# Sliding-window attention in a two-layer hybrid trunk: eight heads per tile, probabilities turned by VectorE and DRAM instead of TensorE

## The chip, the cores and the metric

The kernel runs on one core of a Trainium2 chip. The metric is the device time of one execution in microseconds (us); smaller is better. A core has TensorE (matrix multiply, "PE" in the profile, with "PEld" for its weight loads), VectorE (DVE), ScalarE (ACT), GpSimd (POOL) and SyncE (SP). Each takes its own instructions in the order in which the built program holds them. TensorE writes to PSUM, which here is eight banks of 128 partitions by 512 words; the others work on SBUF and PSUM (POOL on SBUF alone), and SyncE issues nearly all DMAs.

## The reference

Two layers, 1024 tokens, model width 1024, all float32. Each layer projects the normalised input into the inputs of three head groups (windowed attention, retention, gated linear attention), gates each group's output, and projects the concatenation back. The change is in the attention group alone:

```python
ATTN_HEADS = 8; ATTN_KV_HEADS = 2; HEAD_DIM = 64; WINDOW = 128; ATTN_BLOCK = 128
def sliding_window_attention(q, k, v, sinks):          # S = 1024, 8 blocks of 128
    kk, vv = with_prev(kb), with_prev(vb)              # each block sees itself and the one before
    s = jnp.einsum('bnqhgd,bnkhd->bnhgqk', qb, kk) * (D ** -0.5)
    s = jnp.where(valid, s, -1e30)                     # 0 <= i + 128 - j < WINDOW
    p = jax.nn.softmax(jnp.concatenate([s, sink], axis=-1), axis=-1)[..., :-1]
    return jnp.einsum('bnhgqk,bnkhd->bnqhgd', p, vv)
...
a_out = sliding_window_attention(aq, ak, av, sinks) * jax.nn.silu(ag)
y = jnp.concatenate([a_out, r_out, g_out], axis=-1) @ w_out
```

For one query the window holds exactly 128 keys: those above its place in the previous block and those up to its place in its own. So 128 probabilities per query and head are enough, one from each key position, previous or own.

## The kernel before

The tokens are eight tiles of 128 (t = 0 to 7), and two halves (hf) of four tiles. The eight heads are two groups g of four; inside a group the two heads of a pair j lie in partitions 0 to 63 and 64 to 127 (r = 0, 1). A float32 operand is split where precision allows it into a rounded high part and the rest, and a product takes three passes (`PASSES`: high x high, low x high, high x low) in the faster `fp32r` form; transposes and value products run in plain float32.

The order on TensorE is written by a planner inside the kernel: `mult` and `transp` add estimated costs to a clock `clk`, long matrix products call `pump()` every few matmuls, and `pump` lets waiting jobs (generators) go on whose due time has come. A job yields a delay (`lat(key, l)`, from the table `L`, with own values for layer 1 under `@1`) or a flag that another job sets. The planner never waits on the chip: it only decides the order. The other engines' order follows the order of emission, moved by the framework's scheduler where buffers and operands allow it.

Around the attention a layer runs, in this order: the projections of retention and linear attention; key and value projections `do_kv(p)` for tile pairs, with the keys turned by TensorE (`attn_kv`) into `kT`; the rotations `attn_rot(l, hf, g)`, each two projections of 24 matmuls of 512 columns, multiplied by sine and cosine on VectorE, with two 32-partition blocks of each pair exchanged by DMA on SyncE; the gate projections (`gate`, eight in all: two halves, two groups, two k each); and the output projection, which first loads the mixture of a tile (`load_mix`, or parts of it in the last layer's `last_output`, where pairs of tiles share seven products).

In the attention job `attn_q(l, t, g, q)` one group of four heads of one tile goes through: 12 score matmuls into two banks (L911); previous-block scores copied by ACT and own-block scores by VectorE under a mask (L918 to L920); maximum (L922), four exponentials with sums (L925), reciprocal (L928), normalisation on POOL (L929); then, after `aq3`, four TensorE transposes (L934), a copy by ACT, a mask on POOL (L940); after `aq4` the value products (L946), two column halves of TensorE at a time: `va` is v of the previous tile with all probabilities, `vd` the difference of the two tiles' v with the masked ones; a copy and a store to `aoS` in DRAM. q is split into high and low once per half and group, by `split_later`, 5 to 6 us after the rotation, into a tile `mq` of the `mx` ring.

The gates wait for the four tiles of their half and group (flags `ao`), load `aoS` from DRAM, multiply, split, and store to `mixS` (and `mixF` in the last layer); `load_mix` waits for those. Pools: `t2` (128 x 512 words) has B2 = 10 buffers, `t1` B1 = 8, `smx` SMB = 3, and of the eight PSUM banks three are `mm` (projections) and five `aux` (all else).

Of the kernel before, what the change touches and what calls it, by code (L numbers as in the profile page):

```python
# [17 lines left out]
P = 128  # L18
# [42 lines left out]
def host_constants():  # L61
# [9 lines left out]
    c["mask2"] = ((i[:, None] <= i[None, :]) & (i[:, None] // 32 == i[None, :] // 32)).astype(np.int32)  # L71
    c["curmask"] = (i[:, None] >= i[None, :]).astype(np.int32)
# [21 lines left out]
def trunk(ctx: ExitStack, tc: tile.TileContext, ins, cst, out):  # L94
# [167 lines left out]
    srS = dr.tile([NT, P, 256], F32, name="srS")  # L262
    tabS = dr.tile([NP_, P, 2, 256], F32, name="tabS")
# [501 lines left out]
    curmask = cload("curmask", I32)  # L765
    rmask = cload("rmask")
# [74 lines left out]
    def split_later(mq, q, name):  # L841
        yield lat("aq6", name[1])
        for j in range(2):
            split(mq[:, 0, j], mq[:, 1, j], q[j])
        flag(name, lat("aq2", name[1]))

# [12 lines left out]
    def attn_rot(l, hf, g, w_):  # L859
# [15 lines left out]
        q = w  # L875
        for j in range(2):
            A.activation(q[j], u[j], AF.Copy)
            for r in range(2):
                dst, src = 64 * r + 32 * (1 - j), 64 * r + 32 * j
                dma("qst", q[j][dst:dst + 32], u[1 - j][src:src + 32])  # L880
        mq = mix_tile().rearrange("p a k q -> p (a k q)").rearrange("p (a j n) -> p a j n", a=2, j=2)
        kv[(hf, g)] = mq
        job(split_later(mq, q, ("q", l, hf, g)))

    def attn_run(l):

        for hf in range(2):
            for g in range(2):
                for t in range(4 * hf, 4 * hf + 4):
                    yield (lat("aq7" if hf else "aq1", l), ("q", l, hf, g))  # L890
                    yield (0.0, ("kT", l, t))
                    job(attn_q(l, t, g, kv[(hf, g)]))

    def attn_q(l, t, g, q):

        sm = gp.tile([P, 4, 129], F32, tag="smx", name=nm("smx"), bufs=SMB)
        V.tensor_copy(sm[:, :, 128], sink8[:, l, 4 * g:4 * g + 4])
        if t == 0:
            G.memset(sm[:, :, 0:128], -1e30)
        else:  # L900
            vd = gp.tile([P, P], F32, tag="vd", name=nm("vd"), bufs=3)
            G.tensor_tensor(vd, kv["v"][t], kv["v"][t - 1], ALU.subtract)
        pss = [aux(), aux()]
        n = P if t == 0 else 2 * P
        cols = slice((t + 1) * P - n, (t + 1) * P)
        for j in range(2):
            qc = slice(P * (t % 4), P * (t % 4) + P)
            for i, (a, b) in enumerate(PASSES):
                for r in range(2):
                    rr = slice(64 * r, 64 * r + 64)  # L910
                    mult(pss[r][:, j * n:(j + 1) * n], q[rr, a, j, qc], kv["kT"][b][rr, cols],  # L911
                         i == 0, i == 2, n / 4600.0)
        if t % 4 == 3:
            flag(("s", l, t // 4, g))
        for r in range(2):
            pv = pss[r][:, 0:2 * n].rearrange("p (j c n) -> p j c n", j=2, n=P)
            sv = sm[:, r:4:2, 0:128]
            if t > 0:  # L918
                copy("sprev", sv, pv[:, :, 0, :])
            V.copy_predicated(sv, curmask.unsqueeze(1).to_broadcast((P, 2, P)), pv[:, :, n // P - 1, :])  # L920
        mx = small(4)
        V.tensor_reduce(mx, sm, AX.X, ALU.max, negate=True)  # L922
        sums = small(4)
        for h in range(4):
            A.activation(sm[:, h, :], sm[:, h, :], AF.Exp, bias=mx[:, h:h + 1],  # L925
                         accum_out=sums[:, h:h + 1])
        rs = small(4)
        V.reciprocal(rs, sums)  # L928
        eng("pn").tensor_tensor(sm[:, :, 0:128], sm[:, :, 0:128], rs.unsqueeze(2).to_broadcast((P, 4, P)), ALU.mult)  # L929
        yield lat("aq3", l)  # L930

        pp = aux()
        for h in range(4):
            transp(pp[:, h * P:(h + 1) * P], sm[:, h, 0:128], ident)  # L934
# [787 lines left out]
```

## Time and profile before

| what | us |
|---|---|
| median of three runs | 997.67 (996.91 to 997.82) |
| the profiled execution's own time | 996.31 |
| its span, first to last instruction | 994.6 |
| TensorE busy | 965.7 |
| VectorE busy | 683.2 |
| ACT busy | 409.3 |
| POOL busy | 246.3 |

A row of the profile names line, engine, operation, result and operands, the shape, a count, and then busy time in us, mean ns of one, and the idle time of the engine before them with what ended it. In the timeline the first number is the start and the second how long the merged group took; matmuls overlap, so the distance between two starts is the price on TensorE. A window row gives length and busy time of PE, PEld, DVE, ACT and POOL with instruction counts, then granted clock, DMA share and GB/s. A DMA row gives the count, the size, and the median time from issue to landing.

### The profile page before, as it was taken

Reading aid. Unit: us, or ns where it says so; the run is one execution under the profiler, and the core shown is the slowest. Engines: PE = TensorE matmul, PEld = TensorE weight load, DVE = VectorE, ACT = ScalarE, POOL = GpSimd, SP = SyncE. Lnnn points to the kernel's source line nnn. Section 1 sums busy time; section 2 is a strip of 40 time slices with the busy share of each in tenths; the row PEclk is TensorE's granted clock in tenths of the full one; section 3 lists DMA queues with packets and bytes.
Section 4 is the critical chain, followed back from the end, with each engine's and each line's share of the span. In section 5 each row is a group of like instructions: output and inputs, shape, how many; then the busy total and the mean of one; then the engine's idle time right before and its main releaser. Section 6 shows DMA issues by size and latency. Waiting matters only on the chain.

```text
span 994.6 us, 19641 instructions
## 1 busy us (share of the span) xinstructions
PE 965.7 (97%) x7133; PEld 824.3 (83%) x7133; DVE 683.2 (69%) x1679; ACT 409.3 (41%) x1152; POOL 246.3 (25%) x310
## 2 busy tenths in 40 slices
PE   5899999999999999999999999999999999999996
PEld 1599999888998777778889999988999877777785
DVE  3779857677766777664677286775766577567876
ACT  2477312233332656632555332133333257574222
POOL 2322001233310234420124101113322034545000
PEclk8899999999999999999999999999999999999999
DMA  9843513523135355587555241352122434378883
GB/s 321 290 138 97 159 44 115 177 86 121 61 100 166 91 157 168 170 274 239 189 170 171 69 150 38 118 157 83 53 93 86 127 91 133 112 235 266 267 262 139
DMA packets 112305, 148.77 MB, mean 150 GB/s; under 512 B 12065, under 2 KB 63821, under 8 KB 112209
## 3 DMA queue, kind: packets, MB, share of 16 engines
q1 hardware_dynamic: 106512, 137.96, 44.5%
q10 hardware_dynamic: 5696, 9.56, 2.6%
q8 instruction: 56, 0.92, 0.4%
q14 instruction: 41, 0.33, 0.1%
HBM read 109.20 MB, written 36.18 MB: 146 GB/s over the span
## 4 chain that ended last, share of the span: by engine, by line
PE 80%; DVE 7%; DMA 7%; issue 2%; POOL 1%; ACT 1%; SPq 0%; ACTq 0%; POOLq 0%; DVEq 0%
PE mm L165 61%; PE aux L165 14%; PE aux L180 5%; DMA st<-in_w_in_dram 2%; POOL sm L635 1%; DMA t<-aoS 1%; DMA st<-in_w_last_dram 1%; DMA xk<-in_x_dram 1%; DVE arena L533 1%; DMA a<-mixS 1%; DVE t L1248 0%; DVE t L328 0%; DMA t<-in_x_dram 0%; DMA t<-xs 0%; DMA mixS<-t 0%
## 5 line engine op out<-in xcount | busy, mean ns | idle before, releaser
L165 PE MATMUL mm<-arena 128*128 128x256 f32 (+2 forms) x1824 | 299.9, 318 | 1.8 <-ACT arena L704 1.8
L165 PE MATMUL mm<-arena,arena 128*128 128x256 f32 (+2 forms) x1824 | 298.2, 316 | 0.0
L165 PEld LDWEIGHTS mm<-arena 128*128 128x128 f32 x1824 | 255.5, 191 | 26.0 <-issue 3.3
L165 PEld LDWEIGHTS mm<-arena,arena 128*128 128x128 f32 x1824 | 252.2, 188 | 24.3 <-issue 3.7
L635 POOL TENSOR_TENSOR sm<-sm,mhalf 128x1 f32<-128x1 f32 (+1 forms) x64 | 55.8, 872 | 335.9 <-DVE sm L634 317.8
L165 PE MATMUL mm<-arena,mx 128*128 128x512 f32 (+1 forms) x564 | 130.6, 387 | 0.5 <-ACT kept L1341 0.5
L165 PEld LDWEIGHTS mm<-arena,mx 128*128 128x128 f32 x564 | 101.4, 188 | 24.7 <-issue 1.9
L149 ACT ACTIVATE t<-aux 128x256 f32<-128x256 f32 (+2 forms) x124 | 55.8, 468 | 73.8 <-PE aux L180 62.2
L149 ACT ACTIVATE arena<-st 128x512 fp32r<-128x512 f32 x94 | 56.2, 627 | 53.2 <-DMA st<-in_w_in_dram 19.4
L929 POOL TENSOR_TENSOR smx<-smx,sm 128x512 f32<-128x512 f32 x32 | 36.1, 1129 | 125.7 <-DVE sm L928 118.0
L533 POOL TENSOR_TENSOR arena<-st,arena 128x512 fp32r<-128x512 f32 x31 | 42.7, 1378 | 79.7 <-ACT arena L149 72.9
L533 DVE TENSOR_TENSOR arena<-st,arena 128x512 fp32r<-128x512 f32 x77 | 58.0, 775 | 5.2 <-ACT arena L149 3.3
L925 ACT ACTIVATE smx<-smx,sm 128x129 f32<-128x129 f32 x128 | 49.9, 393 | 25.9 <-DVE sm L922 25.7
L364 DVE SCALAR_TENSOR_TENSOR acc<-st,c_act,acc 128x512 f32<-128x512 f32 x60 | 46.7, 778 | 16.9 <-DMA st<-in_w_mod_dram 16.5
L180 PE MATMUL aux<-c_ident,t 128*128 128x128 f32 (+1 forms) x292 | 48.2, 282 | 5.4 <-DVE t L666 5.0
L180 PEld LDWEIGHTS aux<-c_ident,t 128*128 128x128 f32 (+1 forms) x292 | 35.0, 144 | 12.4 <-DVE t L666 6.9
L698 ACT ACTIVATE t<-aux,mod,mod 128x128 f32<-128x128 f32 x68 | 25.9, 459 | 43.0 <-DVE t L1248 18.1
L165 PEld LDWEIGHTS aux<-t,mx 32*128 32x128 f32 (+1 forms) x896 | 39.5, 187 | 3.9 <-issue 2.1
L973 ACT ACTIVATE t<-aux 128x256 f32<-128x256 f32 x32 | 12.3, 383 | 73.6 <-PE aux L165 65.0
L165 PE MATMUL aux<-t,mx 32*128 32x32 f32 (+1 forms) x896 | 40.7, 272 | 0.0
L920 DVE COPY_PREDICATED smx<-c_curmask,aux 128x256 f32<-128x256 int32 x64 | 25.4, 446 | 19.5 <-ACT smx L149 17.2
L1248 DVE SCALAR_TENSOR_TENSOR t<-t,sm,t 128x512 f32<-128x512 f32 x32 | 24.0, 780 | 18.2 <-DMA t<-in_x_dram 10.8
(224 smaller groups left out, 1387.7 us busy)
## 6 DMA issues: line engine op xcount, KB each, us to landing
st<-in_w_in_dram SPq DMA_DIRECT2D x96, 256.0 KB, 3.8
st<-in_w_mod_dram SPq DMA_DIRECT2D x64, 256.0 KB, 3.1
mx<-mixS SPq DMA_DIRECT2D x20, 512.0 KB, 4.9
mixS<-t SPq DMA_DIRECT2D x72, 128.0 KB, 3.7
st<-in_w_last_dram SPq DMA_DIRECT2D x36, 256.0 KB, 3.8
wm<-in_w_mod_dram SPq DMA_DIRECT2D x12, 512.0 KB, 7.0
t<-in_x_dram SPq DMA_DIRECT2D x24, 256.0 KB, 4.9
t<-tabS SPq DMA_DIRECT2D x16, 256.0 KB, 4.6
```

The source lines that it names most:

```text
L149: A.activation(dst, src, AF.Copy)
L165: T.matmul(dst, lhsT, rhs, start=start, stop=stop)
L180: T.transpose(dst, src, idn)
L364: V.scalar_tensor_tensor(acc, wt, c_act[:, k:k + 1], acc, ALU.mult, ALU.add)
L533: e.tensor_tensor(lo, st, f(hi), ALU.subtract)
L635: G.tensor_tensor(r, r, mhalf[:, :w], ALU.pow)
L698: A.activation(hf[:, ks], at[kt], AF.Identity, scale=gain, bias=shift)
L920: V.copy_predicated(sv, curmask.unsqueeze(1).to_broadcast((P, 2, P)), pv[:, :, n // P - 1, :])
L925: A.activation(sm[:, h, :], sm[:, h, :], AF.Exp, bias=mx[:, h:h + 1], accum_out=sums[:, h:h + 1])
L929: eng("pn").tensor_tensor(sm[:, :, 0:128], sm[:, :, 0:128], rs.unsqueeze(2).to_broadcast((P, 4, P)), ALU.mult)
L973: A.activation(sq, po, AF.Square)
L1248: V.scalar_tensor_tensor(xt[j], yg[j], r, xt[j], ALU.mult, ALU.add)
```

## The change

One attention job per tile handles all eight heads. q of a half stays unsplit, all eight heads in one `mx` tile, and each job splits its own 128 tokens into high and low (`qs`, two `t2` tiles). The scores of both groups follow one another (24 matmuls, four banks), then one maximum, eight exponentials and one normalisation. In place of the TensorE transposes VectorE turns the 32 x 32 blocks into `tb`, four DMAs write them to `pS` in DRAM and one DMA reads them back as `pT`, whose partitions are key positions. POOL multiplies by a constant mask `dmask` and forms `vd` by halves. The value products use the four 64 by 64 quarters of TensorE: key positions 0 to 63 and 64 to 127 (c) go to two banks, heads r to two column halves; ACT and VectorE add the two banks. The first half's rotations and the start of the attention job move ahead of the last two `do_kv`. Buffers: `t2` 11, `t1` 7, `smx` 2 of double size, `vd` 1, and `kept` in the last layer alternates between the rings of `smx` and `pT`. Delays: `aq1` 10.5, `aq2` 3.2, `aq6` 7.0, `aq4` 26.0 in both layers; `aq3` and `aq7` are gone.

```diff
+    c["dmask"] = np.concatenate([i[:64, None] > j, i[:64, None] <= j]).astype(f)
...
+    pS = dr.tile([NT, P, 4, 256], F32, name="pS")
...
-        q = w
+        if g == 0:
+            kv[hf] = mix_tile(F32).rearrange("p a k q -> p (a k q)").rearrange("p (k n) -> p k n", k=4)
         for j in range(2):
-            A.activation(q[j], u[j], AF.Copy)
+            q = kv[hf][:, 2 * g + j]
+            A.activation(q, u[j], AF.Copy)
...
-        job(split_later(mq, q, ("q", l, hf, g)))
+        flag(("q", l, hf, g), lat("aq6", l))
...
+        for t in range(NT):
+            yield (lat("aq1", l) if t else 0.0, ("q", l, t // 4, 1))
+            yield (0.0, ("kT", l, t))
+            job(attn_q(l, t, kv[t // 4]))
...
+        qs = [t2(F32R).rearrange("p (k n) -> p k n", k=4) for _ in range(2)]
+        split(*qs, q[:, :, P * (t % 4):P * (t % 4) + P])
+        sm = gp.tile([P, 8, 129], F32, tag="smx", name=nm("smx"), bufs=SMB)
...
+        yield lat("aq2", l)
+        pss = [[aux(), aux()], [aux(), aux()]]
...
+        for g in range(2):
+            for j in range(2):
+                for i, (a, b) in enumerate(PASSES):
+                    for r in range(2):
+                        rr = slice(64 * r, 64 * r + 64)
+                        mult(pss[g][r][:, j * n:(j + 1) * n], qs[a][rr, 2 * g + j], kv["kT"][b][rr, cols],
+                             i == 0, i == 2, n / 4600.0)
...
-        for h in range(4):
+        for h in range(8):
             A.activation(sm[:, h, :], sm[:, h, :], AF.Exp, bias=mx[:, h:h + 1],
                          accum_out=sums[:, h:h + 1])
...
-        yield lat("aq3", l)
-
-        pp = aux()
-        for h in range(4):
-            transp(pp[:, h * P:(h + 1) * P], sm[:, h, 0:128], ident)
-        pf = t2()
-        copy("pf0", pf, pp)
...
+        tb = gp.tile([P, 4, 8, 32], F32, tag="tb", name=nm("tb"), bufs=1)
+        V.transpose(tb.rearrange("p j h b -> p h j b"), sm[:, :, 0:128].rearrange("p h (j b) -> p h j b", j=4))
+        there = pS[t].rearrange("(j a) i n -> i a j n", j=4)
+        for i in range(4):
+            dma("sp", there[i], tb[32 * i:32 * i + 32].rearrange("p j h b -> p j (h b)"))
+        pT = gp.tile([P, 4, 8, 32], F32, tag="pT", name=nm("pT"), bufs=2)
+        dma("lp", pT.rearrange("p i h b -> p i (h b)"), pS[t])
         if t > 0:
+            vd = gp.tile([P, P], F32, tag="vd", name=nm("vd"), bufs=1)
+            pr = t2().rearrange("p (i h b) -> p i h b", i=2, h=8)
...
+                G.tensor_tensor(vd[rr], kv["v"][t - 1 + c][rr], kv["v"][t - c][rr], ALU.subtract)
+                G.tensor_tensor(pr[rr], pT[rr, 2 * c:2 * c + 2], dm[rr], ALU.mult)
         yield lat("aq4", l)
-        po = aux()
...
+        po = [aux(), aux()]
+        for part in range(2 if t else 1):
+            for c in range(2):
+                rr = slice(64 * c, 64 * c + 64)
+                for r in range(2):
+                    cc = slice(64 * r, 64 * r + 64)
+                    d4 = po[c][cc].rearrange("p (h i b) -> p h i b", h=4, i=4)
+                    if part:
+                        mult(d4[:, :, 2 * c:2 * c + 2], vd[rr, cc],
+                             pr[rr, :, r:8:2, :].rearrange("p i h b -> p h i b"), False, True, 0.11)
+                    else:
+                        mult(d4, kv["v"][max(t - c, 0)][rr, cc],
+                             pT[rr, :, r:8:2, :].rearrange("p i h b -> p h i b"), True, t == 0, 0.22)
+        ao = t2()
+        A.activation(ao, po[0], AF.Copy)
+        V.tensor_tensor(ao, po[1], ao, ALU.add)
+        dma("sao", aoS[t], ao.rearrange("p (k q) -> p k q", k=4))
...
-        for p in range(1, NP_):
+        do_kv(1)
+        for g in range(2):
+            attn_rot(l, 0, g, used(l, f"aq{g}"))
+            pump()
+        job(attn_run(l))
+        for p in range(2, NP_):
             do_kv(p)
         load(l, "ag0")
-        job(attn_run(l))
...
-B2, B1, BS, BST, MMB, SMB = 10, 8, 11, 5, 3, 3
+B2, B1, BS, BST, MMB, SMB = 11, 7, 11, 5, 3, 2
...
-    nc = _bacc.Bacc("TRN2", target_bir_lowering=False, num_devices=1)
+    nc = _bacc.Bacc("TRN2", target_bir_lowering=False, num_devices=1, dynamic_dma_scratch_size=1024)
```

99 lines of the change are left out of this document (35 added, 64 removed).

## The prediction

> **What bounds the kernel now.** I read the page's busy shares first, then its chain of waits, then the windows of the stage that the change rewrites.
>
> ```profile
> span 994.6 us, 19641 instructions
> PE 965.7 (97%) x7133; PEld 824.3 (83%) x7133; DVE 683.2 (69%) x1679; ACT 409.3 (41%) x1152; POOL 246.3 (25%) x310
> PE 80%; DVE 7%; DMA 7%; issue 2%; POOL 1%; ACT 1%; SPq 0%; ACTq 0%; POOLq 0%; DVEq 0%
> 375.00:400.00 25.00, 25.00 (x158) 18.66 (x156) 19.05 (x37) 17.49 (x58) 12.27 (x13) 1.00 0.57 179
> 850.00:875.00 25.00, 25.00 (x157) 17.97 (x154) 15.86 (x34) 16.17 (x54) 12.93 (x14) 1.00 0.43 137
> ```
>
> TensorE sets the time. In the attention stages (about 317 to 430 us and 791 to 908 us) it has no idle time at all at full granted clock (1.00), while VectorE is busy 16 to 19 us of 25. So there work taken from TensorE is worth its full time, as long as nothing new makes TensorE wait; a wait costs its full time too. The timeline gives TensorE's prices by the distance between starts:
>
> ```profile
> 390.48 0.60 PE L180 MATMUL aux<-c_ident,smx 128*128 128x128 f32 x4
> 391.01 0.98 PE L165 MATMUL aux<-kT,mx 64*128 64x256 f32 x12
> 391.92 0.65 PE L165 MATMUL aux<-t,va 128*64 128x256 f32 x4
> 392.40 0.60 PE L165 MATMUL aux<-t,vd 128*64 128x256 f32 x4
> 392.93 3.92 PE L165 MATMUL mm<-arena 128*128 128x512 f32 x16
> 396.69 0.60 PE L180 MATMUL aux<-c_ident,smx 128*128 128x128 f32 x4
> 397.05 1.18 PE L165 MATMUL mm<-arena 128*128 128x512 f32 x4
> L165 PE MATMUL mm<-arena 128*128 128x256 f32 x1152 | 151.0, 286 | 0.0
> ```
>
> Four transposes take 0.53 or 0.36 us, the scores of one head group 0.91, its value products 1.01, and a 512-column matmul 3.76/16 = 0.235.
>
> **TensorE: what goes.** The 128 transposes go: 32 groups of about 0.45 = 14 us. Value products: per tile now 2 x 1.01 = 2.02 us, two column halves abreast; then 4 matmuls of 512 columns and 4 of 256. Whether four quarters run abreast no row shows. Half-height scores do run two abreast (256 columns at 0.91/12 = 0.076, full height 151.0/1152 = 0.131). Four abreast give three quarters of today's column time, 1.5 us; two abreast give 3.0. I take 1.5, by the halves: 14 x 0.5 = 7 us. Scores in one block save perhaps 2 us. Sum of the gain: 23 us. Were it two abreast, the product would only fill waits worked out below.
>
> The Trainium skill speaks against the exchange: VectorE: DVE Perf Modes, "The three transpose paths", gives TensorE 390 ns for a 128x128 bf16 transpose, VectorE 311 ns and 32x32 blocks only, and its "Rules for kernel authors" leave the 128x128 transpose to TensorE. The trace has 0.09 to 0.13 us per transpose on TensorE; by the page's figure the removal would be worth an estimated 50 us, so there the trace decides, while its VectorE price is weighed among the rivals.
>
> **What is added to the chain.** Today no VectorE work of one tile is needed by the next tile's scores: q is split once per half and group. The change splits q per tile, and in the built program's order on VectorE the low half of the split of tile t+1 stands behind the block transpose of tile t (tiles 1 to 6, both layers). An engine takes its instructions in order, so the scores of t+1 wait for the whole softmax of t. The rows of this stage:
>
> ```profile
> L920 DVE COPY_PREDICATED smx<-c_curmask,aux 128x256 f32<-128x256 int32 x32 | 12.6, 446 | 11.3 <-ACT smx L149 10.1 <-PE aux L165 1.2
> L922 DVE TENSOR_REDUCE sm<-smx 128x4 f32<-128x516 f32 x15 | 10.3, 685 | 0.2
> L925 ACT ACTIVATE smx<-smx,sm 128x129 f32<-128x129 f32 x60 | 23.4, 392 | 9.4 <-DVE sm L922 9.4
> L149 ACT ACTIVATE smx<-aux 128x256 f32<-128x256 f32 x28 | 9.3, 382 | 9.7 <-PE aux L165 9.7
> L928 DVE RECIPROCAL sm<-sm 128x4 f32<-128x4 f32 x15 | 2.6, 173 | 9.5 <-ACT smx L925 9.5
> L929 POOL TENSOR_TENSOR smx<-smx,sm 128x512 f32<-128x512 f32 x15 | 17.6, 1175 | 64.2 <-DVE sm L928 59.5 <-DVE sm L279 3.2 <-DVE smx L897 1.4
> L533 POOL TENSOR_TENSOR arena<-st,arena 128x512 fp32r<-128x512 f32 x5 | 7.4, 1474 | 11.0 <-ACT arena L149 8.0 <-ACT smx L925 3.0
> L533 DVE TENSOR_TENSOR arena<-st,arena 128x512 fp32r<-128x512 f32 x11 | 8.4, 797 | 0.2
> L524 DVE SCALAR_TENSOR_TENSOR arena<-st,gnc,arena 128x512 fp32r<-128x512 f32 x4 | 4.8, 1192 | 0.0
> L364 DVE SCALAR_TENSOR_TENSOR acc<-st,c_act,acc 128x512 f32<-128x512 f32 x11 | 9.5, 863 | 0.7 <-DMA st<-in_w_mod_dram 0.5
> L870 DVE TENSOR_TENSOR t<-mm,t 128x512 f32<-128x512 f32 x5 | 3.4, 687 | 0.5 <-PE mm L165 0.5
> L873 DVE TENSOR_TENSOR t<-t,t 128x512 f32<-128x512 f32 x3 | 2.9, 955 | 0.0
> L839 DVE TENSOR_TENSOR mx<-t,mx 128x512 fp32r<-128x512 f32 x6 | 4.6, 792 | 0.6 <-ACT mx L838 0.6
> L151 DVE CAST arena<-st 128x512 fp32r<-128x512 f32 x5 | 2.1, 420 | 0.4 <-PE mm L165 0.4
> L897 DVE COPY smx<-sink 128x4 f32<-128x4 f32 x14 | 4.2, 299 | 3.7 <-PE aux L180 3.6
> L1584 DVE SCALAR_TENSOR_TENSOR t<-t,mm 128x512 f32<-128x512 f32 x8 | 5.5, 682 | 1.5 <-ACT t L1583 1.4
> ```
>
> From the end of a tile's scores to the end of its block transpose: two of the four copies on ACT and the last masked copy 1.4 (the first two banks are ready earlier); the maximum over 8 heads 1.3 (0.685 doubled, less one start); eight exponentials at 23.4/60 = 0.39, 3.1, and the last sum 0.2; reciprocal 0.2; normalisation on POOL, twice 1.175 less a start, 2.2; the transpose of 1024 words per partition, which no row shows, between two casts (0.84) and two subtractions (1.6), I take 1.3, nearer the subtractions since it is 32-bit; hand-overs 0.5. Sum **10.2 us**, with bounds 8.9 and 11.5. TensorE has 40 to 44 matmuls of 0.235 and one set of value products to do between two scores: about **10.7 us**. So the chain alone would just fit. What does not fit is the VectorE work that stands between the transpose and the low half: rotation, weight subtractions, modulation sums, gate and output additions, and the low half itself (0.79). By the built order and these rows, for tiles 1-2, 2-3, 3-4, 4-5, 5-6:
>
> - layer 0: 7.6, 8.6, 2.5, 6.2, 5.7 (the first is a sink copy 0.3, a cast 0.42, two subtractions 1.6, four products from PSUM 2.7, two combinations 1.8, the low half 0.8);
> - layer 1: 9.2, 5.7, 2.5, 4.8, 8.5.
>
> Together 61.3; ten times (10.2 + 0.1 - 10.7) takes 4 off. On POOL the normalisation of tile 4 stands behind the masked product of tile 3, which needs tile 3's probabilities back: stores 1.8, landing 2.4, issue 0.5, load 4.9, product 2.0 and a weight subtraction 1.5 make 13.0 after the transpose, against 10.4 when tile 4 is ready: 2.6 in each layer. **Ten gaps: 62 us.** The stage pays this on TensorE, since everything behind the scores in its order waits too.
>
> **What is moved.** The first half's two rotations (four 24-matmul projections, their eight products and four combinations on VectorE, four table loads and eight partition moves on SyncE) go ahead of the last four key and value projections. Instructions and bytes stay the same. The weights of the gates' first unit (ag0) now have two rotations less ahead of their use: 4 x 24 x 0.235 = 22.6 us of cover where there were 45, for four loads that land in 3.8 us each. I cost this at nothing; without that cover it would be some 5 us. The mask constant and the kept tiles' buffers: nothing, one small load and a new name.
>
> ```profile
> st<-in_w_in_dram SPq DMA_DIRECT2D x96, 256.0 KB, 3.8
> ```
>
> **The DMA trips.** One issue on SyncE takes 0.93/2 = 0.46 us below. The landings come from the list of DMA issues; the other rows show how the before crosses the same path on SyncE's queue.
>
> ```profile
> aoS<-t SPq DMA_DIRECT2D x32, 128.0 KB, 2.4
> t<-aoS SPq DMA_DIRECT2D x16, 256.0 KB, 5.4
> mixS<-t SPq DMA_DIRECT2D x16, 256.0 KB, 3.5
> mx<-mixS SPq DMA_DIRECT2D x20, 512.0 KB, 4.9
> 393.46 0.33 SPq L154 DMA_DIRECT2D aoS<-t  x1
> 397.44 0.93 SPq L154 DMA_DIRECT2D t<-aoS  x2
> 403.21 2.11 SPq L154 DMA_DIRECT2D mixS<-t  x3
> 410.16 0.32 SPq L154 DMA_DIRECT2D mx<-mixS  x1
> 423.34 3.99 PE L165 MATMUL mm<-arena,mx 128*128 128x512 f32 x16
> ```
>
> From the value products of the last tile of the first half (end 392.93) to the mixture in SBUF (410.16 + 4.9) the before needs 22 us, and TensorE asks for it after 30.4. The change joins all eight heads to one tile, so the last tile of a half comes later, and it puts each probability store and load on SyncE, where the store waits for the transpose and the load for the store's landing; all that is queued behind waits too.
>
> - Layer 0, tile 7: the output store of tile 3 stands behind the probability load of tile 5, so it goes 5.2 us after that transpose, lands at 7.6, and the gate's loads land at 13.0. VectorE has the first gate product ahead of tile 6's maximum, which was ready at 8.6. Tile 6's transpose ends at 22.5, then 7.5 of gate splits: scores of tile 7 at 30.1 where TensorE was ready at 17.2: 13 us.
> - The mixture's stores stand behind tile 6's probability load: last issue 31.3, landing 3.5, load 5.3: 40.1, TensorE ready at 31.5: 9 us.
> - Layer 1, tile 7: the gate's loads themselves stand behind tile 6's probability load; they land 11.8 after that transpose, and 14 us of gate and weight work precede the low half: 25 us. The first mixture load: 7 us.
> - Second half, layer 0: value products of tile 7, 1.4 to the store, 2.6, loads 7.2, products and splits to 17.4, stores 3.9, load 5.3: 26.6, cover 80 matmuls and eight transposes, 19.7: 7 us. Layer 1: a load that waits for TensorE's next 24 matmuls stands ahead of the store: 31 against 84 matmuls, 19.7: 11 us.
>
> Together **72 us**. VectorE's, ACT's and POOL's other changes (ACT loses about 1.4 us a tile) lie inside these waits and cost nothing more.
>
> **Sum.** The profiled execution took 996.31 us with a span of 994.6, against a median of 997.67. 996.3 - 23 + 62 + 72 = 1107, with the median's 1.4 about 1108; I say **1105 us**, as idle queues should shorten some landings. Bounds: chain 8.9, other prices 15% lower and DMA waits a third shorter leave +55 (1053); chain 11.5 and each landing 1 us longer give +148 (1145).
>
> **The rivals.**
>
> 1. *The DMA waits alone.* If the low half were done during the softmax's idle moments, the 62 us fall away: 1105 - 62 = 1043. For it: VectorE is busy only 16 to 19 us of 25. Against it: the built order is what the engine follows. Chance 0.15.
> 2. *A slower turn and longer trips.* A block transpose of 2.5 us, about two of the 1.192 us rows, lengthens each of 14 gaps by 1.2, 17 us; stores in 1 KB pieces that land 1 us later add some 6: 1128. The stage's DMA share of 0.57 leaves room for the added 16 MB, which speaks against it. Chance 0.14. The 311 ns of the Trainium skill (the page and section named above), eight times per tile, are an estimated 2.5 us and would give this same time; no run here shows it yet.
> 3. *The gain arrives.* The queues keep up, TensorE stays as full as in the windows above, and only the 23 us go: 974. It decides once chain and following VectorE work end within the 10.7 us of cover; with 2.5 to 9.2 us of such work the chain would have to take 2 to 8 us, where its exponentials and POOL product alone need 5.3. For it: the before also strings these engines together and never lets TensorE wait here. Chance 0.04.
> 4. *The edit does less than it says*: quarters two abreast. The longer products lie inside the gaps, so 1105 stays within 5 us; it belongs to the forecast.
>
> **How the numbers follow.** Forecast 0.66, rival 1 0.15, rival 2 0.14, rival 3 0.04, something between 0.01. The range 1045 to 1140 leaves out the third rival, most of the first one's lower tail and the far end of the second. Measurement cannot tell less than 0.2% from no change: faster 0.04, same 0.01, slower 0.95.
>
> **What would show it.** In the changed profile the two attention stages should be some 50 to 70 us longer with TensorE idle 5 to 9 us ahead of most scores, released by the low half of the split (VectorE) or ACT's high half; the distance from scores to scores should be 13 to 20 us, not 11; the largest single gap should be ahead of tile 7's scores in layer 1; the block transpose should take 0.8 to 1.6 us; a set of value products 1.5 us. Wrong I am if TensorE is idle less than 40 us in all, if gaps ahead of scores are under 2 us, or if the waits are named after probability loads at the value products, which here have 25 us.

## The result and the profile after

The changed kernel took 1154.45 us (median of four runs, 1151.97 to 1156.04) against 997.75 us before: a ratio of 1.1565, 95% interval 1.1535 to 1.1596. The direction was as forecast; the size was 49 us above the forecast and 14 above the range.

The page of the changed kernel: its span, its busy shares and the granted clock in forty slices; the second view is the clock of the kernel before.

```profile
span 1154.2 us, 19345 instructions
PE 977.1 (85%) x7005; PEld 835.2 (72%) x7005; DVE 712.0 (62%) x1663; ACT 389.3 (34%) x1104; POOL 259.5 (22%) x292
PEclk8899999999997888598999999999999798858889
```

```profile
PEclk8899999999999999999999999999999999999999
```

TensorE has fewer instructions and is busy 11 us longer; its idle time went from 994.6 - 965.7 = 28.9 to 1154.2 - 977.1 = 177.1 us. The clock row, all 9 before but for the first slices, has dips in both attention stages. What TensorE waited for, over the whole run (line, releaser: us in total, times, longest):

```profile
PE aux L167 <- ACT t L842: 70.1, 7, 29.2
PE aux L167 <- DVE t L843: 41.6, 9, 9.3
PE mm L167 <- DMA mx<-mixS: 13.8, 4, 7.6
PE aux L182 <- DVE t L669: 12.4, 5, 4.1
PE mm L167 <- DVE t L1358: 8.1, 1, 8.1
...
PE mm L167 <- DMA a<-mixS: 4.0, 1, 4.0
```

L842 and L843 are the high and the low half of the split of q: 70.1 + 41.6 = 111.7 us of waits ahead of scores. The rows of TensorE's timeline show them, all but the last in layer 0 (start, length, engine, line, shape, and in brackets the idle time before):

```profile
356.04 0.58 PE L167 MATMUL aux<-kT,t 64*128 64x256 f32 x2 [6.09 <-ACT t L842]
363.88 2.72 PE L167 MATMUL aux<-kT,t 64*128 64x256 f32 x22 [7.25 <-DVE t L843]
...
409.17 1.09 PE L167 MATMUL aux<-pT,va 64*64 64x512 f32 x8
410.08 0.61 PE L167 MATMUL aux<-t,vd 64*64 64x256 f32 x8
410.62 4.80 PE L167 MATMUL mm<-arena 128*128 128x512 f32 x20
...
444.16 2.72 PE L167 MATMUL aux<-kT,t 64*128 64x256 f32 x22 [5.12 <-DVE t L843]
...
476.09 3.44 PE L167 MATMUL aux<-kT,t 64*128 64x256 f32 x24 [17.85 <-ACT t L842]
1033.75 3.44 PE L167 MATMUL aux<-kT,t 64*128 64x256 f32 x24 [29.20 <-ACT t L842]
```

The two largest waits stand ahead of tile 7's scores, the larger in layer 1. The other kT waits make 111.7 - 17.9 - 29.2 = 64.6 us for tiles 2 to 6 of both layers. One tile's value products take from 409.17 to 410.62, 1.45 us. After a wait the 22 matmuls left of a tile's scores take 2.7 us; all 24 without a wait take 1.7. The granted clock differs too, in windows of 1 us, the first in the wait that ends at 444.16 (length, busy time of PE, PEld, DVE, ACT, POOL, then granted clock, DMA share, GB/s):

```profile
443.00:444.00 1.00, 0.00 (x0) 0.00 (x0) 1.00 (x2) 0.00 (x0) 0.00 (x0) 0.50 0.73 154
...
448.00:449.00 1.00, 1.00 (x4) 0.81 (x3) 0.12 (x1) 0.00 (x0) 0.00 (x0) 0.50 0.70 272
449.00:450.00 1.00, 1.00 (x5) 0.78 (x5) 0.00 (x0) 0.00 (x0) 0.97 (x1) 0.82 0.22 82
```

The clock is at 0.50 during the wait and stays there for 5 us of work behind it. Laid over the trace's clock record, which lists each stretch at a lower clock, TensorE was busy 94.4 us at 0.50 (10.8 before), so 47.2 - 5.4 = 42 us of its time were lost to the lower clock.

VectorE's timeline shows the end of one tile's chain (tile 5 of layer 0); the block transpose waits for POOL, and the low half (L843) stands behind it and seven other items:

```profile
437.78 1.25 DVE L928 STREAM_TRANSPOSE tb<-smx 128x1024 f32<-128x1024 f32 x1 [2.08 <-POOL smx L926]
...
443.43 0.68 DVE L843 TENSOR_TENSOR t<-mx,t 128x512 fp32r<-128x512 f32 x1
```

### The profile page after: what moved, and what is told of

It reads as the page before. It is cut to its first block, busy times and chain, and to the rows that moved or that the text cites. A ratio compares the mean times of both kernels' runs of the same rounds, so it can differ in the third digit from the quotient of the medians.

```text
span 1154.2 us, 19345 instructions
## 1 busy us (share of the span) xinstructions
PE 977.1 (85%) x7005; PEld 835.2 (72%) x7005; DVE 712.0 (62%) x1663; ACT 389.3 (34%) x1104; POOL 259.5 (22%) x292
## 5 line engine op out<-in xcount | busy, mean ns | idle before, releaser
L167 PEld LDWEIGHTS mm<-arena 128*128 128x128 f32 x1824 | 259.2, 193 | 27.5 <-issue 3.7
L167 PEld LDWEIGHTS mm<-arena,arena 128*128 128x128 f32 x1824 | 256.1, 191 | 26.8 <-issue 4.2
L167 PE MATMUL mm<-arena,mx 128*128 128x512 f32 (+1 forms) x564 | 141.0, 409 | 21.9 <-DMA mx<-mixS 13.8
L167 PEld LDWEIGHTS mm<-arena,mx 128*128 128x128 f32 x564 | 109.5, 203 | 48.3 <-issue 8.8
L167 PE MATMUL aux<-kT,t 64*128 64x256 f32 (+1 forms) x384 | 42.9, 383 | 112.0 <-ACT t L842 70.1
L167 PEld LDWEIGHTS aux<-kT,t 64*128 64x128 f32 x384 | 36.2, 274 | 120.8 <-ACT t L842 73.5
L536 POOL TENSOR_TENSOR arena<-st,arena 128x512 fp32r<-128x512 f32 x31 | 43.1, 1391 | 145.9 <-ACT arena L151 127.6
L922 ACT ACTIVATE smx<-smx,sm 128x129 f32<-128x129 f32 x128 | 49.7, 390 | 41.6 <-DVE sm L919 41.6
L536 DVE TENSOR_TENSOR arena<-st,arena 128x512 fp32r<-128x512 f32 x77 | 58.4, 780 | 8.5 <-ACT arena L151 5.6
L941 POOL TENSOR_TENSOR t<-pT,c_dmask 64x512 f32<-64x512 f32 x28 | 39.9, 1426 | 105.1 <-DMA pT<-pS 104.1
L182 PE MATMUL aux<-c_ident,t 128*128 128x128 f32 (+1 forms) x292 | 49.8, 290 | 15.9 <-DVE t L669 12.4
L367 DVE SCALAR_TENSOR_TENSOR acc<-st,c_act,acc 128x512 f32<-128x512 f32 x60 | 47.0, 783 | 25.4 <-DMA st<-in_w_mod_dram 24.8
L182 PEld LDWEIGHTS aux<-c_ident,t 128*128 128x128 f32 (+1 forms) x292 | 35.8, 147 | 24.8 <-DVE t L669 11.3
L926 POOL TENSOR_TENSOR smx<-smx,sm 128x1024 f32<-128x1024 f32 x16 | 30.8, 1922 | 82.7 <-DVE sm L925 77.0
L151 ACT ACTIVATE t<-aux 128x256 fp32r<-128x256 f32 (+2 forms) x60 | 25.4, 442 | 61.3 <-PE aux L182 61.2
L928 DVE STREAM_TRANSPOSE tb<-smx 128x1024 f32<-128x1024 f32 x16 | 19.9, 1244 | 34.0 <-POOL smx L926 34.0
```

The source lines that it names most:

```text
L151: A.activation(dst, src, AF.Copy)
L167: T.matmul(dst, lhsT, rhs, start=start, stop=stop)
L182: T.transpose(dst, src, idn)
L367: V.scalar_tensor_tensor(acc, wt, c_act[:, k:k + 1], acc, ALU.mult, ALU.add)
L536: e.tensor_tensor(lo, st, f(hi), ALU.subtract)
L928: V.transpose(tb.rearrange("p j h b -> p h j b"), sm[:, :, 0:128].rearrange("p h (j b) -> p h j b", j=4))
```

## The experiments

Times are medians beside runs of the kernel before on the same chip (997 to 998 us); intervals are 95% of the ratio to it. First the changed kernel with one suspected cause taken away at a time.

**The low half taken off the chain.** Each job splits the next tile's q:

```diff
-        split(*qs, q[:, :, P * (t % 4):P * (t % 4) + P])
+        qs = kv.pop("qs", None) or qsplit(t)
+        if t + 1 < NT and flags.get(("q", l, (t + 1) // 4, 1), 1e9) - 3.0 <= clk[0]:
+            kv["qs"] = qsplit(t + 1)
```

> Each tile's q is split into high and low one tile earlier, so that no low half stands behind the block transpose of the tile before. Order theory (the scores of t+1 wait for the softmax and transpose of t because the low half stands behind them on VectorE): the ten gaps ahead of the scores of tiles 2 to 6, 33.1 us in layer 0 and 31.6 us in layer 1, go almost wholly, the gaps ahead of tile 7 and of the mixture products stay: 1075 to 1090 us. Rival (VectorE is late anyway: the masked copies of t+1 stand behind the transpose of t, so banks and softmax buffers come free late): the wait turns up elsewhere, 1130 us or more.

1137.50 us (1.1373 to 1.1449): only 17 us less. The waits for the split are gone; others have taken their place, by this run's list of TensorE's waits (15.6 us more stand ahead of scores, for masked copies, L923):

```profile
PE mm L167 <- DMA mx<-mixS: 62.1, 4, 30.6
PE mm L167 <- DVE t L1607: 22.5, 6, 6.1
PE mm L167 <- DVE t L869: 16.9, 2, 8.5
```

Gate (L1607) and rotation (L869) now read projection banks late, masked copies (L923) score banks, and the mixture comes late. The low half ended the waits, but taking it away removed little of their cost. Gate, rotation and copies stand in the same queue of VectorE as the transposes; why the mixture is later was not separated (the edit also holds two `t2` buffers one tile longer).

**The waits filled with work.** Matmuls of the identity, overwritten by the scores behind them:

```diff
         pss = [[aux(), aux()], [aux(), aux()]]
+        for _ in range([[0,0,56,17,9,28,23,79],[0,0,65,12,0,17,39,130]][l][t]):
+            nc.tensor.matmul(pss[0][0][:, 0:P], ident, ident, start=True, stop=True)
```

> Matmuls of the identity, whose result is overwritten, stand on TensorE ahead of the scores, about as many as the wait there is long (9 to 130 of some 0.21 us); nothing else changes. Clock theory in full (all work lost at granted clock 0.50 in the eleven stretches from 353 to 487 us and 906 to 1047 us comes back, 29 us): 1125 us with granted clock 1.00 in these stages. Clock theory with a loop (inside the run of tiles only the scores themselves, 2.6 to 2.7 us against 1.7 to 1.8, are in the loop score, softmax, transpose, low half, score; the projections between only wait longer): ten times 0.9 and some 8 us behind the two tiles 7: about 1137 us. Rival (the lower clock costs nothing, it falls into waits): 1154 us.

1157.83 us (1.1534 to 1.1679), no shorter. In its trace the scores of eight of the ten tiles 2 to 6 are back at 1.7 to 2.0 us (from 2.7 to 3.3), none of them was kept back by the added matmuls, and the time at clock 0.50 falls from 189 to 104 us. Yet tile 1 to tile 6 (low half to low half) takes 109.8 and 100.3 us in place of 107.8 and 102.3: three of the ten steps are 1.0 to 1.4 us shorter, the others equal or longer. Inside the run of tiles the lower clock is covered on the whole: VectorE's order, with what it waits for, sets the pace. Behind tile 7 the clock fell to 0.50 here too, so this run does not test it there.

**The probabilities' transfers on other queues** (ACT's, ACT's with the earlier split, POOL's):

```diff
-"sp": "S", "lp": "S"
+"sp": "A", "lp": "A"      (third run: "P", "P")
```

> The stores and loads of the probabilities are issued by ACT in place of SyncE. Queue theory (gate loads, output and mixture stores are late because they stand on SyncE behind stores that wait for a transpose): the gaps ahead of tile 7 (17.9 and 29.2 us) and ahead of the mixture products fall by half or more: 1110 to 1125 us. Rival (ACT then waits for the transpose and the landing itself, so exponentials, high halves and copies come later): the gaps between tiles grow by 2 to 4 us each, 1150 to 1190 us.

> The split one tile earlier and the probabilities' transfers on ACT together. If the two causes add: 1030 to 1060 us. If ACT's own waits for the transpose are a cost, or the two overlap: not below the earlier split alone by more than 10 us, 1070 to 1090 us.

> The stores and loads of the probabilities are issued by POOL in place of SyncE, behind its own normalisation and ahead of its masked products, which wait for them anyhow. Queue theory (SyncE's waits make the gate loads, the stores and the table loads late): gaps ahead of tile 7 and the mixture products (73 us) fall by half, 1110 to 1125 us. Rival (the gaps come from VectorE's order, the queue only shows it): 1145 to 1165 us.

1180.84 (1.1803 to 1.1870), 1151.88 (1.1496 to 1.1584) and 1166.19 us (1.1680 to 1.1715): 26, 14 and 12 us more than with SyncE; the second is above both of its ranges, the third just above its rival's. The engine that issues the load stands until the stores have landed (behind one load in layer 0 ACT was idle for 7.8 us, ahead of one POOL for 4.2), and ACT and POOL have the next softmax to do. No run gave the trip a queue without other work. The remedy from the other side, output, gate and mixture transfers on ACT (`sao`, `lao`, `smh`, `sml`) with the earlier split:

> The split one tile earlier (1137.5 us alone), and the output stores, gate loads and mixture stores issued by ACT, so that they no longer stand on SyncE behind stores that wait for a block transpose. Queue theory (the 62 us in which TensorE waits for mixture loads there come from SyncE's order): 1085 to 1105 us. Rival (they come from VectorE's and ACT's order, value products and gates are late by themselves): 1130 to 1150 us.

1149.36 us (1.1476 to 1.1547), 12 more than the earlier split alone, as the rival had it.

**The normalisation on VectorE** (`"pn": "V"`):

> The normalisation of the probabilities goes from POOL (1.92 us) to VectorE itself, so that the block transpose follows without a wait for another engine. If the wait of VectorE for POOL (34.0 us ahead of 16 transposes) is on the path: some 10 to 25 us less than 1154, the product itself costing VectorE 16 times about 1.3 us. If it is hidden behind the exponentials: 1154 to 1170 us.

1144.93 us (1.1462 to 1.1516), 9.5 us less, just under the first range: a small part of the chain.

**The rotation tables of the second half loaded by ACT.** From tile 1's transpose to tile 2's low half the changed kernel needs 13.3 us in layer 0 where the forecast had 7.6. SyncE's timeline there shows the table load right behind tile 1's stores, which waited for its transpose, and load:

```profile
350.57 1.78 SPq L156 DMA_DIRECT2D pS<-tb  x4
...
354.84 0.33 SPq L156 DMA_DIRECT2D pT<-pS  x1
355.26 0.90 SPq L862 DMA_DIRECT2D t<-tabS  x2
```

```diff
-            nc.sync.dma_start(d.rearrange("p (s n) -> p s n", s=2),
+            (A if hf else nc.sync).dma_start(d.rearrange("p (s n) -> p s n", s=2),
```

> The changed kernel with the second half's rotation tables loaded by ACT in place of SyncE. From the transpose of tile 1 to the low half of tile 2 the prediction had 7.6 and 9.2 us, the changed trace has 13.3 and 14.2, with VectorE idle 7.1 us for a table load. If the table load stands on SyncE behind the probability stores: that stretch falls by 4 to 6 us in each layer and the time by 6 to 12 us, 1142 to 1149 us. If the loads are late for another reason (buffers): 1152 to 1158 us.

1154.51 us (1.1531 to 1.1602): unchanged. The stretch fell to 11.3 and 13.3 us (from 13.3 and 14.2), less than expected, and nothing of it reached the end. In layer 1 the tables are hardly the matter: of VectorE's idle time in that stretch 5.4 us end with loads of the last layer's weights (L574) and 0.5 with the tables. In this run ACT issues the last loads only behind its own exponentials, at 347.3 to 351.3 us; an unhindered load was not tried.

Next, the parts of the change apart.

**The trip left out.** The block transpose writes `pT` directly; stores, load and the exchange of blocks are left out.

```diff
-        tb = ...; V.transpose(tb, ...); dma("sp", ...) x4; dma("lp", pT, pS[t])
+        V.transpose(pT.rearrange("p j h b -> p h j b"), sm[:, :, 0:128]...)
```

> The block transpose stays on VectorE, but its result is used as it is: the exchange of blocks through DRAM (four stores and a load per tile) is left out, so the values are wrong. If the trip and SyncE's queue behind it make most of the turn's 106 us: 1055 to 1085 us. If VectorE standing at the transpose makes it: 1120 to 1150 us.

1100.72 us (1.0996 to 1.1082): 54 us less, between the two ranges. Half of the turn's cost is the trip, half stays with a transpose on VectorE and no transfer at all. Its list of TensorE's waits shows where the trip was paid:

```profile
PE aux L167 <- ACT t L842: 47.1, 5, 22.1
PE aux L167 <- DVE t L843: 18.0, 9, 3.6
PE mm L167 <- DMA mx<-mixS: 15.8, 4, 9.0
PE mm L167 <- DVE t L1353: 7.7, 1, 7.7
PE mm L167 <- DMA a<-mixS: 4.2, 1, 4.2
```

Mixture and pair products still wait 15.8 + 7.7 + 4.2 = 27.7 us (25.9 with the trip), and tile 7's scores 13.4 in layer 0 and 22.1 + 1.8 in layer 1, 37.3 in all (47.1). The waits ahead of tiles 2 to 6 fall from 64.6 to 27.8 us. VectorE's timeline of this run has the low halves of tiles 1 and 6 here:

```profile
332.67 2.05 DVE L843 TENSOR_TENSOR t<-mx,t 128x512 fp32r<-128x512 f32 x1
419.51 0.67 DVE L843 TENSOR_TENSOR t<-mx,t 128x512 fp32r<-128x512 f32 x1
850.62 2.05 DVE L843 TENSOR_TENSOR t<-mx,t 128x512 fp32r<-128x512 f32 x1
937.82 0.68 DVE L843 TENSOR_TENSOR t<-mx,t 128x512 fp32r<-128x512 f32 x1
```

From one to the other it takes 85.5 and 85.8 us, with the trip 107.8 and 102.3: 38.8 us of the 54. Tile 1's transpose to tile 2's low half takes 7.0 us in both layers. What VectorE waited for between these low halves, with the trip (two lines of layer 0, one of layer 1) and without it (one of each):

```profile
DVE acc L367 <- DMA st<-in_w_mod_dram: 12.3, 3, 5.9
DVE t L868 <- DMA t<-tabS: 7.1, 1, 7.1
DVE st L574 <- DMA st<-in_w_last_dram: 8.9, 4, 3.4
```

```profile
DVE acc L367 <- DMA st<-in_w_mod_dram: 3.7, 2, 2.6
DVE st L574 <- DMA st<-in_w_last_dram: 2.2, 1, 2.2
```

So much of the 38.8 us is weights and tables that reach VectorE late: its waits for loads fall by some 23 us when SyncE has no trip to serve. That the loads are late because they are issued behind the stores and loads of the trip fits SyncE's order above; a run that moves them all was not made.

**TensorE's turn back, eight heads and quarters kept**, and the same with the earlier split:

```diff
-        tb = ...; V.transpose(tb, ...); dma("sp", ...) x4; dma("lp", pT, pS[t])
+        yield 10.5
+        pp = [aux(), aux()]
+        for h in range(8):
+            transp(pp[h // 4][:, (h % 4) * P:(h % 4) * P + P], sm[:, h, 0:128], ident)
+        for g in range(2):
+            A.activation(pT[:, :, 4 * g:4 * g + 4]..., pp[g]..., AF.Copy)
-        yield lat("aq4", l)
+        yield 8.0
```

> The eight heads of a tile stay in one job, with the split per tile and the values in four quarters, but the probabilities are turned by eight TensorE transposes and two copies of ACT, as before: no block transpose on VectorE, no trip through DRAM, 16 us more of TensorE work. Theory (the turn is the cause: VectorE stands at the block transpose until POOL has normalised, and SyncE behind the stores): the waits go, about 990 to 1010 us. Rival (one softmax of eight heads in place of two of four is the cause: VectorE waits for eight exponentials in a row with nothing to do, the low half stands behind): most of the waits stay, 1080 us or more.

> As the run before, and the split of q one tile earlier. If the low half still costs in that run: 10 to 40 us less than it. If the turn is the whole cause: the same within 5 us, 985 to 1010 us.

1048.21 (1.0494 to 1.0537) and 1044.37 us (1.0416 to 1.0533), the first between its two ranges. The turn makes 106 of the 157 us, though TensorE does 128 transposes again; 50 us are something else, and the low half is not it (4 us, inside the intervals).

**The turn alone**, on the kernel before with four heads per job, values in halves, `aq4` 24:

> The kernel before with the turn alone: jobs of four heads, the early split, values in halves, but the probabilities turned by VectorE in blocks and through DRAM, value products 24 us of the planner's clock after the scores. Known so far: before 997.7, eight heads with TensorE's turn 1048, both 1154 us. If the two effects add, the turn costs 1154 - 1048 = 106 us here too: about 1095 to 1110 us. If it costs this much only with one softmax in flight (with two half-size ones VectorE has the other group's work while it stands): 1000 to 1045 us.

1063.36 us (1.0628 to 1.0690), between the two ranges: the turn costs 66 us in the kernel with two small softmaxes in flight, 106 in the one with one large softmax. With the earlier split in both, 1137.5 - 1044.4 = 93 us is the fairer partner of the 66. The two kernels also differ in buffers, in the order of the rotations and in the quarters, so that the number of softmaxes makes the difference is likely, not shown.

**The quarters alone**, on the kernel before (with one `t1` buffer more):

```diff
-        po = aux()
-        ... mult(po[64 * r:64 * r + 64, 0:256]..., vt[:, 64 * r:64 * r + 64], h4(pvv)[:, r:4:2, :], ...)
-        copy("aoc", ao, po[:, 0:256])
+        po = [aux(), aux()]
+        ... mult(po[c][cc, 0:256]..., kv["v"][max(t - c, 0)][rr, cc], h4(pf)[rr, r:4:2, :], ...)
+        A.activation(ao, po[0][:, 0:256], AF.Copy)
+        V.tensor_tensor(ao, po[1][:, 0:256], ao, ALU.add)
```

> The kernel before with the values in four quarters alone (and one more addition on VectorE and smaller masks on POOL per group). By the changed trace a tile's value products take 1.45 us on TensorE in place of 2.02: 14 tiles, 8 us, 988 to 992 us. If the added step or the second bank makes TensorE wait, 996 to 1003 us.

1018.15 us (1.0172 to 1.0230): 20 us slower, and above both ranges. Its counterpart, eight heads with TensorE's turn and halves (one bank, one mask over all partitions, in the buffer that `tb` leaves free), without and with the earlier split:

> Eight heads and TensorE's turn as in the run with 1048 us, but the value products in two column halves as before: one bank, no addition on VectorE, one mask on POOL over all 128 partitions; TensorE has 8 us more to do. If the quarters cost here what they cost alone (20 us, through the second bank and POOL): 1025 to 1040 us. If eight heads at once make the loss: 1048 to 1060 us.

> Eight heads, TensorE's turn, values in halves (1024 us), and the split of q one tile earlier. What is left there is 26 us over the kernel before, with 10.5 us of TensorE waits for the low half. If the low half is a good part of what eight heads cost: 1005 to 1014 us. If the waits move to the next thing that VectorE brings late, as they did in the changed kernel: 1018 to 1026 us.

1023.95 (1.0233 to 1.0298) and 1022.73 us (1.0219 to 1.0273). The quarters cost 24 us here, against 20 alone; the earlier split once more wins nothing, as its second range had it. POOL's rows name one added cost: in the kernel with quarters a mask is two products over 64 partitions, with halves one selection over 128, here a row of each in turn:

```profile
L942 POOL TENSOR_TENSOR t<-pT,c_dmask 64x512 f32<-64x512 f32 x28 | 41.1, 1468 | 13.2 <-ACT pT L933 12.0
```

```profile
L939 POOL TENSOR_SCALAR_AFFINE_SELECT pr<-pT 128x1024 f32<-128x1024 f32 x14 | 21.4, 1528 | 22.0 <-ACT pT L933 22.0
```

**Another bank for the quarters** (`MMB` 2 in place of 3, so six banks for scores, transposes and values):

> Eight heads, TensorE's turn and the quarters (1048 us), with six PSUM banks in place of five for scores, transposes and values, and two in place of three for the projections. Scores hold four of these banks and the quarters need two, halves one; in that profile TensorE waits ahead of value products for VectorE's masked copies. If the missing bank is what the quarters cost (24 us over the halves): 1025 to 1035 us. If it is POOL's masks and the addition, or the two projection banks are too few: 1045 us or more.

1061.03 us (1.0609 to 1.0641), 13 us slower than with five. It does not tell whether the second bank costs, because the projections lost one: 13.2 us of waits for the gate (L1602) to read a projection bank are new. This stays open.

**The waits of the kernel with TensorE's turn filled**, at the places that the expectation names:

> The kernel with eight heads and TensorE's own turn (1048 us), with matmuls of the identity (results overwritten) at eleven places where TensorE waits 2 to 6 us there: scores of tiles 3 and 7, value products of tile 3, three products of the last layer's second pair. That profile has 31 us of TensorE work lost at granted clock 0.50 against 5 before, and products that take 4.6 to 5.5 us in place of 2.9 behind such waits. If the lower clock is on the path there (TensorE sets the pace between the waits): 1026 to 1036 us. If it is covered as in the filled run of the changed kernel: 1045 to 1050 us.

1054.83 us (1.0554 to 1.0629), not less, and above both ranges. TensorE is idle 15.6 us less than without the filling and loses 17 us to the clock in place of 31, but the identity matmuls are some 36 us of work, more than both together. One tail can be compared by itself. TensorE's timeline in the last layer, without the filling and then with it:

```profile
958.84 5.60 PE L167 MATMUL mm<-arena,ma 128*128 128x512 f32 x24
968.36 5.46 PE L167 MATMUL mm<-arena,mx 128*128 128x512 f32 x12 [3.91 <-DVE t L1359]
983.67 4.58 PE L167 MATMUL mm<-arena,mx 128*128 128x512 f32 x12 [4.00 <-DVE t L1359]
992.39 5.46 PE L167 MATMUL mm<-arena,a 128*128 128x512 f32 x12 [4.14 <-DMA a<-mixS]
```

```profile
969.69 5.60 PE L167 MATMUL mm<-arena,ma 128*128 128x512 f32 x24
979.82 3.00 PE L167 MATMUL mm<-arena,mx 128*128 128x512 f32 x12
993.41 3.01 PE L167 MATMUL mm<-arena,mx 128*128 128x512 f32 x12
1000.41 2.99 PE L167 MATMUL mm<-arena,a 128*128 128x512 f32 x12
```

The three products lose 6.5 us in all, and the tail from the end of the `ma` products to the last matmul shrinks from 72.3 to 67.5 us, in one profiled execution of each. In this tail, where TensorE waits ahead of these three products alone, the clock is on the path.

**The smaller scratch space alone** (`dynamic_dma_scratch_size=1024` on the kernel before):

> The kernel before with the one setting of the change that no trace row shows, the smaller scratch space for dynamic DMAs, which the runs of the parts share. If it costs nothing: 996 to 999 us. If it holds DMAs up, the runs of the parts owe some of their loss to it: 1003 us or more.

997.79 us, ratio 1.0002 (0.9985 to 1.0019): nothing.

The ladder of parts:

| kernel | us | step |
|---|---|---|
| before | 997.7 | |
| eight heads per job, TensorE's turn, halves (and the change's order, delays and buffers) | 1024.0 | +26 |
| and quarters | 1048.2 | +24 |
| and VectorE's turn without the trip (blocks not exchanged) | 1100.7 | +52 |
| and the trip: the changed kernel | 1154.5 | +54 |
| before with quarters alone | 1018.2 | +20 |
| before with the turn alone | 1063.4 | +66 |

The moved rotations, the new delays and the new buffers were not run by themselves; their share of the 26 us is open. No version beat the kernel before.

## Why the prediction was wrong, point by point

**The bound: right.** TensorE set the time before, and each new wait was paid in full.

**The waits: right in place, and in size partly by luck.** Ahead of tiles 2 to 6 it had 62 us, measured 64.6; ahead of tile 7 13 and 25, measured 17.9 and 29.2, the largest where it said; for mixture and pair products 34, measured 13.8 + 8.1 + 4.0 = 25.9. Together 134 against 138. TensorE's whole idle time grew by 148; the longer waits for the layer norm (L669, 12.4 us) were not foreseen. But in the run of tiles TensorE's waits came out as forecast although the run itself did not: it took 23.5 us longer, of which 15.6 went into work at clock 0.50 and 5 into more work of TensorE than the forecast had there.

**The run of tiles: undersized.** These rows of VectorE's timeline are the low halves of tiles 1 and 6 in both layers:

```profile
334.30 2.05 DVE L843 TENSOR_TENSOR t<-mx,t 128x512 fp32r<-128x512 f32 x1
443.43 0.68 DVE L843 TENSOR_TENSOR t<-mx,t 128x512 fp32r<-128x512 f32 x1
886.34 2.05 DVE L843 TENSOR_TENSOR t<-mx,t 128x512 fp32r<-128x512 f32 x1
989.97 0.68 DVE L843 TENSOR_TENSOR t<-mx,t 128x512 fp32r<-128x512 f32 x1
```

443.43 + 0.68 - 336.35 = 107.8 and 990.65 - 888.39 = 102.3 us. The forecast's terms (5 x (1.8 + 10.2), the work behind the transposes, 2.6 for POOL) give 93.2 and 93.3: 23.5 us short. The stretches to tile 7's scores were 37.1 us after tile 5's transpose in layer 0 (forecast 30.1) and 29.0 after tile 6's in layer 1 (25.8): 10 us short. The chain's own items were no longer than forecast (maximum 1.23 us for 1.3, normalisation 1.92 for 2.2, block transpose 1.25 for 1.3). But from the scores' end to the transpose's end tiles 1 to 5 took 9.3 to 13.7 us, on the mean 11.6, not 10.2: in the two longest of layer 0 the maximum ends 6.4 and 6.9 us after the scores, because VectorE first stands 5.2 and 5.9 us at a sum that waits for a weight load (L367). Nor does one term come out of its own rows: 40 to 44 matmuls of 0.235 and 1.5 us of value products are 10.9 to 11.8 us of cover, not 10.7, and the trace has about 11.3 at full clock.

**The trip: the step that failed.** The forecast put 72 us of waits at the ends of the halves (tile 7, mixture and pair products) down to the trip and SyncE's queue, and gave the trip 2.6 us a layer in the run of tiles. Left out, the trip gives 54 us back, in the main elsewhere: the run of tiles falls from 210.0 to 171.3 us, less than the forecast's 186.5, and the stretches from tile 6's low half to tile 7's by 6.8 and 7.6 us, 53 us together. At the ends of the halves TensorE still waits 65.0 us of 73.0 without any trip. With TensorE's turn (1048 us) the same places wait 21.6 us, so most of what stays comes with the transpose on VectorE. By which step is open; ahead of tile 7 in layer 0 ACT's high half last waits, with and without the trip, for VectorE's splits of the gate (some 3 us; L1619 in the changed kernel), work that the forecast counted too. That SyncE's queue could be relieved by another one did not hold: ACT's and POOL's were slower.

**TensorE's gain of 23 us: the second step that failed.** It was priced at full clock, and a lower clock was put at nothing. Transposes and value products are as cheap as it said (1.45 us a tile for 1.5), yet TensorE is busy 11 us longer, because 42 us of it go to clock 0.50 behind the new waits. On TensorE's account this is the larger error: busy +11 in place of -23, idle +148 in place of +134, 34 + 14 of the 49 us. On the path it is not all clock, for in the run of tiles the lower clock is covered (the filled run). Behind the waits for tile 7, mixture and pair products the clock record has 16 us of it in the two layers, and the tail above shows three such products lose 6.5. 23.5 + 10 + 16 = 50 us is the size of the miss (8 us less at the mixture and pair products and 7 more at the layer norm all but cancel); the 16 us as path time is worked out from the trace, and only its like in the other kernel was measured. Nor are the quarters a gain as built: alone they cost 20 us. What of this is the second bank, the addition or POOL's longer masks was not separated.

**The split as cause: wrong.** Rival 1 had the 62 us fall away if the low half came early. Done early, 17 us fell away. The sum treated the item that ends a wait as its price, when the queue behind the transposes held several items ready to end the next one.

**Rival 2** had a block transpose of 2.5 us and stores that land 1 us later; the transpose takes 1.244 us, and the stores land after 2.3 (`aoS` before: 2.4). The Trainium skill (VectorE: DVE Perf Modes, "The three transpose paths") gives 311 ns for 128x128 in bf16, eight times that are an estimated 2.5 us; the float32 transpose of the trace differs, and the measurement decides. Rival 3 is excluded. Rival 4 (quarters two abreast) falls on TensorE's side, 1.45 us a set.

## What to carry to other kernels

An engine's queue, not the item that ends a wait, is what to price: take the item away alone and see which one ends the wait next. Leave a suspected transfer out in a run of its own and compare the waits place by place, for its cost may sit elsewhere than the queue suggests. Work taken from the bound engine and put into a softmax chain is paid in latency, and here less of it was covered with one large chain than with two small ones (93 to 106 us for 66). Price what a stall does to the bound engine behind it, and a faster product form together with the bank, addition and masks that it needs.

## What the hardware showed that was not expected

The clock can fall after a short wait. In these windows of the changed kernel, TensorE idles 1.58 us of the first and then works at 0.50 for 3.4 us, from 196.8 by the clock record; in the kernel before a wait of 1.29 us at the same place left it at 1.00:

```profile
194.00:196.00 2.00, 0.42 (x4) 0.05 (x2) 0.42 (x1) 1.39 (x3) 0.79 (x1) 1.00 0.95 277
196.00:198.00 2.00, 2.00 (x12) 1.59 (x13) 0.76 (x2) 0.00 (x0) 0.48 (x1) 0.69 0.98 355
198.00:200.00 2.00, 2.00 (x6) 1.55 (x5) 0.00 (x0) 0.00 (x0) 0.00 (x0) 0.50 0.68 180
```

The stretches at 0.50 in the clock record last 3.4, 6.8, 10.2 us and so on. The Trainium skill (TensorE: Matmul & The Clock Gate, "What's actually happening") has a free-running window of 3413 ns, with which these lengths agree; its advice to keep idle gaps under about 3 us ("Why this matters for your kernels") was not enough here.

POOL's products did not get shorter with fewer partitions: in the changed kernel one over 64 x 512 took 1.426 us on the mean (the mask, L941) and one over 128 x 512 1.391 (L536). So a mask as two products over half of the partitions cost 2 x 1.468 = 2.9 us a tile, where one selection over 128 x 1024 took 1.528.
